# The down projection as seven block products with weight sums grown by accumulating loads

## The chip, the cores and the metric

The kernel runs on one core of a Trainium2 chip. Its time is the device time of one execution in microseconds (us). The kernel before was timed three times: median 670.09 us, from 669.1 to 670.38. The profile is of one further execution of 670.29 us; its span, from the first instruction to the last, is 668.5 us.

## The reference

One decoder layer in float32, 512 tokens by 1024 channels: two kinds of attention, a SwiGLU block of width 2816 and a last normalisation. The change concerns the last two lines:

```python
hn = rms_norm(h, norm2_g)
h = h + (silu(hn @ w_gate) * (hn @ w_up)) @ w_down      # (512 x 2816) @ (2816 x 1024)
return rms_norm(h, norm_f_g)
```

## The kernel before

TensorE multiplies numbers of a shortened float32 type (F32R). To keep float32 precision, each operand is split in two: a high part, a cast on ScalarE, and a low part, the difference, on VectorE. Three matmuls (high x high, high x low, low x high) then stand for one.

The gate and up products run first, in 22 units of 128 hidden channels (`first_part`, `second_part`, `third_part`, lines 716 to 746). Each unit already uses seven half-size products; its last one (the weights called `d`, line 744) adds into a bank that VectorE must have read before. The results lie in 22 tiles `zs`, 128 hidden channels by 512 tokens each: four tiles of four, whose names in the rows begin with `act`, and one of six named `h1t`. The operands of gate and up lie in the tiles `X10`, `X11`, `X20` and `X21`, which become free when the last unit has read them. The residual h1 waits in DRAM as `h1d`.

The down projection (lines 781 to 828) goes through the 22 row blocks in order. `down_step(k)` loads 128 rows of the weights (512 KB, SyncE), splits them (`split2`, 128x1024), splits `zs[k]` (`split_g`, 128x512), and issues eight cells, four token blocks by two column halves, each three matmuls of 128x128 by 128x512 into its own PSUM bank. All eight banks gather at once. The last four row blocks (`LAST`) are done cell by cell, so that a cell can be evicted (line 838: bank x 1/rms + h1), squared and, for the first half of a row, multiplied by the gain (line 842) while TensorE goes on. Then the row's root is taken (`rsqrt`) and the two halves are scaled and stored.

A scheduler orders the instructions of each engine from its own model of times; within `manual_schedule` the named engines keep the order of the code, here VectorE and ScalarE in the down projection. Each engine and each queue of transfers works in order, so a waiting instruction holds all behind it. Tiles with the same name share `bufs` buffers in turn: split weights `hl2` three, raw weights `raw2` six, `xe` and `xf` four, `w_hl` five, `w_raw` three.

Of the kernel before, what the change touches and what calls it, by code (L numbers as in the profile page):

```python
# [28 lines left out]
NJ = FFN // P  # L29
EPS = 1e-6  # L30
BIG = 1e30
TW = 640
WC = 512
RB = 32
LAST = 4
# [17 lines left out]
def tile_hybrid_layer(ctx: ExitStack, tc: tile.TileContext, xT, w_qk0, w_t, w_av, w_vb, w_o, w_gu, w_d,  # L53
                      rel, pos2, cw1, cb1, cw2, gT, gf_row, oh, cmask, out):
    nc = tc.nc
# [8 lines left out]
    def bank(tag):  # L64
        return psum.tile([P, 512], F32, name=tag, bufs=BANKS[tag])
# [476 lines left out]
    for step in PLAN.split():  # L542
        n, i = step[0], step[1:]
# [34 lines left out]
    def raw2():  # L578
        return ff.tile([P, 2, WC], F32, name="raw2", bufs=BUFS["raw2"])

    def split2(raw, hi, lo, w=None):

        if w is None:
            w = ff.tile([P, 2, 2, WC], F32R, name="hl2", bufs=BUFS["hl2"])
        copy(hi, w[:, 0], raw)
        tt(lo, w[:, 1], raw, w[:, 0].bitcast(F32), ALU.subtract)
        return w

    def raw1():
        return ws.tile([P, WC], F32, name="w_raw", bufs=BUFS["w_raw"])  # L590
# [151 lines left out]
    def third_part(j, u):  # L742
        y, z = u["y"], zs[j]
        product(u["A"], u["w"]["d"], X2, 4, False)
        tt("v", z[:, :HS], u["A"], y[:, :HS], ALU.mult)
        tt("v", z[:, HS:], z[:, HS:], y[:, HS:], ALU.mult)

    es = []
    for f in range(KT):
# [28 lines left out]
    third_part(NJ - 1, units[NJ - 1])  # L778


    GT = [ff.tile([P, n, S], F32R, name=tag, bufs=1) for n, tag in ((4, "X10"), (4, "X11"), (10, "X20"), (10, "X21"))]
    GH = [GT[0][:, k] for k in range(4)] + [GT[2][:, k] for k in range(10)] + [GT[3][:, k] for k in range(8)]
    GL = [GT[1][:, k] for k in range(4)]
    def w_down(k, w=None):
        raw = raw2()
        nc.sync.dma_start(raw, w_d[k * P:(k + 1) * P, :].rearrange("p (a n) -> p a n", a=2))
        return split2(raw, *ENG["d"], w)

    def split_g(k):
        if k % 4 == 0 and k:  # L790
            q = act.tile([P, 4, S], F32R, name=quads[k // 4 - 1]) if k < 20 else GT[3][:, 8:]
            GL.extend(q[:, i] for i in range(min(4, NJ - k)))
        copy("a", GH[k], zs[k])
        tt("v", GL[k], zs[k], GH[k].bitcast(F32), ALU.subtract)

    def down(ps, t, c, k, w):
        tk = slice(t * P, (t + 1) * P)
        mm3x(ps[c][t], GH[k][:, tk], GL[k][:, tk], w[:, :, c], slice(0, HD), k == 0, k == NJ - 1)

    ps = [[bank(n) for n in ("S", "S", "proj", "proj")], [bank(n) for n in ("PT", "PT", "PT", "O")]]  # L800
    def h1_back(t):
        if t % 2 == 0:
            h1r.append(ff.tile([P, 2, D], F32, name=("X10", "X11")[t // 2], bufs=1))
        nc.sync.dma_start(h1r[t // 2][:, t % 2], h1d[t])

    def cell(t, c):
        return h1r[t // 2][:, t % 2, c * HD:(c + 1) * HD]

    h1r, gf, ws_last, wx = [], [], [], []
    def down_step(k):  # L810
        if k < NJ - LAST:
            w = w_down(k)
        elif k < NJ - 2:
            ws_last.append(w_down(k))
        else:
            if k == NJ - 2:
                wx.append(ff.tile([P, 2, 2, 2, WC], F32R, name="X20", bufs=1))
            ws_last.append(w_down(k, wx[0][:, k - NJ + 2]))
        split_g(k)
        if k < NJ - LAST:  # L820
            for c in range(2):
                for t in range(NT):
                    down(ps, t, c, k, w)
        if k in (1, 2):
            gf.append(ff.tile([P, HD], F32, name="g", bufs=BUFS["g"]))
            nc.sync.dma_start(gf[-1], gf_row[:, (k - 1) * HD:k * HD].to_broadcast([P, HD]))
        if k in (7, 9, 11, 13):
            h1_back((k - 7) // 2)
# [4 lines left out]
    for t in range(NT):
        for c in range(2):
            for i, k in enumerate(range(NJ - LAST, NJ)):
                down(ps, t, c, k, ws_last[i])
            x = cell(t, c)
            nc.vector.scalar_tensor_tensor(out=x, in0=ps[c][t], scalar=nrstd_t[:, t:t + 1], in1=x, op0=ALU.mult,
                                           op1=ALU.add)
            square(t, c, x)  # L840
            if c == 0:
                tt(ENG["c"], x, x, gf[0], ALU.mult)
        rsqrt(slice(t, t + 1), rstd_t)
# [85 lines left out]
```

## Time and profile before

| | us |
|---|---|
| median of three runs | 670.09 |
| the profiled execution, and its span | 670.29, 668.5 |
| TensorE busy | 641.3 |
| VectorE busy | 477.3 |
| ScalarE busy | 352.9 |
| GpSimd busy | 144.3 |

Busy times are unions over the span and say nothing of which engine another waits for; that is read stage by stage. In the rows PE is TensorE, DVE VectorE, ACT ScalarE, POOL GpSimd and SP SyncE; L95 is line 95 of the kernel, and a helper's line stands for all its callers, so groups are told apart by tile names. Matmuls are pipelined: the duration shown for one (0.40 us) is longer than the distance to the next, and the distance is what counts. The same holds in small for VectorE, whose next instruction starts before the last has ended.

### The profile page before, as it was taken

How to read it: one execution, taken by the hardware profiler on the slowest of the kernel's cores; microseconds unless marked ns; L12 is line 12 of the kernel's file. 1: busy time of each engine (PE TensorE's matmuls, PEld its weight loads, DVE VectorE, ACT ScalarE, POOL GpSimd, SP SyncE). 2: the span in 40 equal slices, each digit the busy share in tenths (PEclk: the TensorE clock that was granted, in tenths of full speed). 3: DMA queues.
4: the chain of work that ended last, by engine and by line, in shares of the span. 5: the costliest groups of instructions: out<-in, count | busy, mean ns of one | idle time of the engine just before them, and what ended most of it. 6: DMA issues, size and time to landing. Idle time of an engine off the chain costs nothing.

```text
span 668.5 us, 11164 instructions
## 1 busy us (share of the span) xinstructions
PE 641.3 (96%) x3942; PEld 571.3 (85%) x3942; DVE 477.3 (71%) x994; ACT 352.9 (53%) x745; POOL 144.3 (22%) x184
## 2 busy tenths in 40 slices
PE   9999997999999999987999999999999999999995
PEld 6878887878878887866899999999999988888884
DVE  4458777678787679559899899999998724333355
ACT  5543565345775678558774455545545504222234
POOL 7635842153446645330000000000000000000000
PEclk9999999989999999888899999999999999999998
DMA  6666665446225640063433133323324417222003
GB/s 191 216 177 190 174 176 155 123 140 172 90 95 158 199 150 17 1 206 117 179 128 124 69 111 126 111 95 111 111 96 147 175 58 245 102 94 95 0 2 126
DMA packets 45316, 84.44 MB, mean 126 GB/s; under 512 B 6811, under 2 KB 10139, under 8 KB 45260
## 3 DMA queue, kind: packets, MB, share of 16 engines
q1 hardware_dynamic: 44684, 82.67, 39.1%
q10 hardware_dynamic: 576, 1.05, 0.4%
q8 instruction: 31, 0.51, 0.3%
q14 instruction: 25, 0.20, 0.1%
HBM read 68.45 MB, written 7.64 MB: 114 GB/s over the span
## 4 chain that ended last, share of the span: by engine, by line
PE 78%; DVE 8%; ACT 4%; DMA 4%; issue 3%; SPq 2%; POOL 1%; DVEq 0%; ACTq 0%; POOLq 0%
PE proj L89 8%; PE proj L91 8%; PE proj L90 8%; PE S L90 6%; PE S L89 6%; PE S L91 6%; PE PT L340 3%; PE PT L96 2%; PE PT L95 2%; PE PT L97 2%; PE O L356 2%; PE proj L96 2%; PE proj L95 2%; PE proj L97 2%; PE S L317 2%
## 5 line engine op out<-in xcount | busy, mean ns | idle before, releaser
L76 DVE TENSOR_TENSOR hl<-raw,hl 128x1024 fp32r<-128x1024 f32 x64 | 78.0, 1220 | 61.1 <-ACT hl L71 60.8
L71 ACT CAST hl<-raw 128x1024 fp32r<-128x1024 f32 x64 | 67.3, 1053 | 76.8 <-PE O L97 57.1
L84 POOL TENSOR_TENSOR w_hl<-w_raw,w_hl 128x512 fp32r<-128x512 f32 (+1 forms) x47 | 61.4, 1309 | 61.7 <-ACT w_hl L71 31.5
L71 ACT CAST w_hl<-w_raw 128x512 fp32r<-128x512 f32 (+2 forms) x76 | 43.3, 576 | 58.0 <-PE S L91 18.9
L325 ACT ACTIVATE P<-P,mn 128x512 f32<-128x512 f32 (+1 forms) x96 | 53.5, 559 | 13.3 <-DVE mn L323 13.0
L337 POOL TENSOR_SCALAR P<-P,den 128x512 f32<-128x512 f32 (+1 forms) x96 | 51.4, 554 | 41.4 <-DVE den L329 21.5
L76 DVE TENSOR_TENSOR PTl<-PT,PTh 128x512 fp32r<-128x512 f32 (+2 forms) x96 | 43.7, 482 | 10.2 <-ACT PTh L350 9.9
L323 DVE CUSTOM_DVE_ANT_0 P<-S,T 128x512 f32<-128x512 f32 (+1 forms) x96 | 44.0, 483 | 9.8 <-PE S L318 7.6
L89 PE MATMUL S<-X,hl 128*128 128x256 f32 x176 | 49.9, 284 | 0.7 <-ACT xf L721 0.7
L90 PE MATMUL S<-X,hl 128*128 128x256 f32 x176 | 50.0, 284 | 0.3 <-DVE X L76 0.3
L89 PE MATMUL S<-X,w_hl 128*128 128x256 f32 x176 | 49.7, 284 | 0.5 <-ACT xf L732 0.5
L350 ACT CAST PTh<-PT 128x512 fp32r<-128x512 f32 (+2 forms) x96 | 38.2, 426 | 22.7 <-PE PT L340 18.8
L90 PE MATMUL S<-X,w_hl 128*128 128x256 f32 x176 | 49.8, 283 | 0.0
L91 PE MATMUL S<-X,hl 128*128 128x256 f32 x176 | 49.7, 282 | 0.0
L91 PE MATMUL S<-X,w_hl 128*128 128x256 f32 x176 | 49.7, 283 | 0.0
L89 PE MATMUL proj<-xh,w_hl 128*128 128x512 f32 x112 | 45.6, 408 | 0.5 <-DVE va L282 0.4
L71 ACT CAST w_hl<-raw 128x512 fp32r<-128x512 f32 x45 | 27.3, 619 | 35.5 <-PE S L91 28.3
L90 PE MATMUL proj<-xl,w_hl 128*128 128x512 f32 x112 | 44.7, 399 | 0.0
L91 PE MATMUL proj<-xh,w_hl 128*128 128x512 f32 x112 | 44.6, 398 | 0.0
L84 DVE TENSOR_TENSOR w_hl<-w_raw,w_hl 128x512 fp32r<-128x512 f32 (+1 forms) x37 | 27.4, 747 | 15.7 <-ACT w_hl L71 14.4
L340 PE MATMUL PT<-ident,P 128*128 128x128 f32 x240 | 36.8, 277 | 0.8 <-POOL P L337 0.8
L89 PEld LDWEIGHTS S<-X,hl 128*128 128x128 f32 x176 | 33.9, 193 | 1.1 <-ACT xf L721 1.1
(316 smaller groups left out, 1965.1 us busy)
## 6 DMA issues: line engine op xcount, KB each, us to landing
raw<-in_w_gu_dram SPq DMA_DIRECT2D x46, 256.0 KB, 3.3
raw<-in_w_d_dram SPq DMA_DIRECT2D x22, 512.0 KB, 3.3
w_raw<-in_w_gu_dram SPq DMA_DIRECT2D x42, 256.0 KB, 2.7
w_raw<-in_w_t_dram SPq DMA_DIRECT2D x28, 256.0 KB, 2.8
T<-gd SPq DMA_DIRECT2D x64, 64.0 KB, 1.9
w_raw<-in_w_o_dram SPq DMA_DIRECT2D x16, 256.0 KB, 3.1
w_raw<-in_w_vb_dram SPq DMA_DIRECT2D x16, 140.0 KB, 2.2
Qb<-in_xT_dram SPq DMA_DIRECT2D x8, 256.0 KB, 2.8
```

Source lines behind the costliest of these rows:

```text
L71: nc.scalar.copy(out, in_)
L76: engines[e].tensor_tensor(out=out, in0=in0, in1=in1, op=op)
L84: engines[lo].tensor_tensor(out=w[:, 1, :n], in0=raw[:, :n], in1=w[:, 0, :n].bitcast(F32), op=ALU.subtract)
L89: nc.tensor.matmul(ps, w[:, 0, sl], xh, start=first, stop=False, skip_group_check=skip)
L90: nc.tensor.matmul(ps, w[:, 0, sl], xl, start=False, stop=False, skip_group_check=skip)
L91: nc.tensor.matmul(ps, w[:, 1, sl], xh, start=False, stop=last, skip_group_check=skip)
L95: nc.tensor.matmul(ps, xh, w[:, 0, sl], start=first, stop=False)
L323: nc.vector.tensor_tensor_reduce(out=pp, in0=sv, in1=T[:, S - w:], op0=ALU.add, op1=ALU.min, scale=1.0, scalar=3e38, accum_out=mn[:, t:t + 1])
L325: nc.scalar.activation(pp, pp, AF.Exp, bias=mn[:, t:t + 1], scale=-1.0, accum_out=den[:, t:t + 1])
L337: nc.gpsimd.tensor_scalar(pp, pp, den[:, t:t + 1], 1.0, op0=ALU.mult, op1=ALU.mult)
L340: nc.tensor.transpose(pv[:, kb * P:(kb + 1) * P], pp[:, kb * P:(kb + 1) * P], ident)
L350: nc.scalar.copy(ov[0], pv)
```

## The change

The 2816 hidden channels are cut into an upper and a lower eleven row blocks, the tokens and the output columns into halves. Instead of eight block products, seven are computed, one after the other, each over eleven row blocks for two token blocks and one column half (two banks). Their operands are sums of blocks. All sums on the side of the hidden values (`s1` to `s4`) are made in place on VectorE between the splits. The sums of the weights have plus signs alone. Most are made by loads that GpSimd issues and that add into the tile where it stands (`add_w`, `accum_op`); the rest (`t3`, and `t2` for the last two pairs of row blocks) are VectorE additions. The bank sums go into the residual tile `x0[2]` by evictions (`evict`) that add or subtract. Row blocks are taken in pairs, five pairs and a single one, a step each. TensorE and GpSimd now keep the code's order as well, and SyncE's loads are ordered by hand, too. The loads of the gain (`gf`) stand at their end.

```diff
-    ps = [[bank(n) for n in ("S", "S", "proj", "proj")], [bank(n) for n in ("PT", "PT", "PT", "O")]]
-        for k in range(NJ):
-            down_step(k)
+    HJ = NJ // 2
+    PAIRS = [slice(k, min(k + 2, HJ)) for k in range(0, HJ, 2)]
...
+    with tc.manual_schedule(engines={mybir.EngineType.SP}):
+        r11 = [raw2() for _ in PAIRS]
+        B11 = r11[:5] + [r11[5][:, 0:1]]
+        load_w(B11, 0, 0)
+        x0 = [ff.tile([P, n, WC], F32, name=tag, bufs=1)
+              for n, tag in ((4, "X10"), (4, "X11"), (10, "X20"), (10, "X21"))]
+        B21 = [x0[k // 2][:, 2 * (k % 2):2 * (k % 2) + 2] for k in range(4)] + [x0[2][:, 8:10], r11[5][:, 1:2]]
+        load_w(B21, 1, 0)
+        for t in range(NT):
+            nc.sync.dma_start(x0[2][:, 2 * t:2 * t + 2], h1d[t].rearrange("p (c n) -> p c n", c=2))
+        B22 = [x0[3][:, 2 * k:2 * k + 2] for k in range(5)] + [raw1()[:, None]]
+        load_w(B22, 1, 1)
+        B12 = [ws.tile([P, 2, WC], F32, name="w_hl", bufs=BUFS["w_hl"]) for _ in range(5)] + [raw1()[:, None]]
+        load_w(B12, 0, 1)
+        gf = [ff.tile([P, HD], F32, name="g", bufs=BUFS["g"]) for _ in range(2)]
...
+    def s1(k):
+        minus("v", A21[k], A21[k], A22[k])
...
+    def add_w(kh, ch):
+        def f(k):
+            for i in range(B11[k].shape[1]):
+                nc.gpsimd.dma_start(B11[k][:, i], rows_w(kh, ch, k, i), accum_op=ALU.add)
+        return f
+    def t2(k):
+        if k < 4:
+            add_w(1, 1)(k)
         else:
+            tt("v", B11[k], B11[k], B22[k], ALU.add)
+    def t3(k):
+        tt("v", B12[k], B12[k], B22[k], ALU.add)
...
+    products = [
+        (ps_a, A11, B11, True, (s3, add_w(0, 1)), [(ps_a, 0, 0)], []),
+        (ps_b, A12, B21, True, (s1,), [(ps_b, 0, 0)], [(0, 0), (1, 0)]),
+        (ps_c, A21, B11, True, (s2, t2), [(ps_c, 1, 1)], []),
+        (ps_a, A21, B11, False, (s4, add_w(1, 0)), [(ps_a, 0, 1, -1)], []),
+        (ps_c, A12, B22, False, (t3,), [(ps_c, 0, 1)], [(0, 1), (1, 1)]),
+        (ps_a, A11, B12, False, (), [(ps_a, 1, 1, -1), (ps_a, 1, 0)], [(2, 1), (3, 1)]),
+        (ps_b, A22, B11, True, (), [], [])]
...
+        copy("a", gh[:, :m], a)
+        minus("v", gl[:, :m], a, gh[:, :m].bitcast(F32))
+        copy("a", w[:, 0, :m], b)
+        minus("v", w[:, 1, :m], b, w[:, 0, :m].bitcast(F32))
...
+            parts = prepare(n, k)
+            for f in products[n][4]:
+                f(k)
+            if n == 6 and k >= 3:
+                last.append((k, *parts))
+            else:
+                for i in range(2):
+                    multiply(n, i, k, *parts)
+            if x == 0:
+                last_product(NJ - 1, units[NJ - 1])
+            if n and k == 2:
+                for e in products[n - 1][5]:
+                    evict(*e)
+            if n and k == 3:
+                for c in products[n - 1][6]:
+                    close(*c)
...
+        final(1)
+        square(3, 0, cell(3, 0))
+        store(2)
+        root(r3)
+        gain(3)
+        unroot(r3)
+        scale(3)
+        store(3)
```

What VectorE does in order changes most. In the middle of the down projection before, it alternates between the low part of hidden values (`act<-act,X`) and that of a row block's weights (`hl<-raw,hl`):

```order
L76 TENSOR_TENSOR act_6598<-act_3771,X_6453 128x512
L76 TENSOR_TENSOR hl_6627<-raw_6625,hl_6627 128x1024
L76 TENSOR_TENSOR act_6598<-act_3771,X_6453 128x512
L76 TENSOR_TENSOR hl_6658<-raw_6656,hl_6658 128x1024
L76 TENSOR_TENSOR act_6598<-act_3771,X_6453 128x512
L76 TENSOR_TENSOR hl_6689<-raw_6687,hl_6689 128x1024
```

In the third product of the change, from its fourth step on, `xf<-act,xe` and `hl<-raw,hl` are the splits of hidden values and weights, L848 and `raw<-raw,X` sums, and `X<-X,g` the two gain multiplies:

```order
L75 TENSOR_TENSOR xf<-act_3771,xe 128x512
L75 TENSOR_TENSOR hl_6843<-raw_6448,hl_6843 128x1024
L848 SCALAR_TENSOR_TENSOR act_3771<-h1t,act_3771 128x2x256
L75 TENSOR_TENSOR X_6464<-X_6464,g 128x512 x2
L75 TENSOR_TENSOR xf<-act_3772,xe 128x512
L75 TENSOR_TENSOR hl_6871<-raw_6449,hl_6871 128x1024
L848 SCALAR_TENSOR_TENSOR act_3772<-h1t,act_3772 128x2x256
L75 TENSOR_TENSOR raw_6449<-raw_6449,X_6465 128x1024
L75 TENSOR_TENSOR xf<-act_3772,xe 128x256
L75 TENSOR_TENSOR hl_6892<-raw_6450,hl_6892 128x512
```

Between two weight splits now stand sums, and the gain multiplies have moved from the end of the kernel into the middle of the stage.

SyncE's queue before, from the third weight block of the down projection on, with the two gain loads (`g<-in_gf_dram`) among the weights:

```order
L786 DMA raw_6529<-in_w_d_dram 128x1024
L786 DMA raw_6562<-in_w_d_dram 128x1024
L786 DMA raw_6593<-in_w_d_dram 128x1024
L786 DMA raw_6625<-in_w_d_dram 128x1024
L786 DMA raw_6656<-in_w_d_dram 128x1024
L826 DMA g<-in_gf_dram 128x512
L786 DMA raw_6687<-in_w_d_dram 128x1024
L786 DMA raw_6720<-in_w_d_dram 128x1024
L826 DMA g<-in_gf_dram 128x512
L786 DMA raw_6752<-in_w_d_dram 128x1024
```

And after, where `X_6462` to `X_6465` are X10, X11, X20 and X21:

```order
L813 DMA raw_6450<-in_w_d_dram 128x512
L813 DMA X_6462<-in_w_d_dram 128x512 x4
L813 DMA X_6463<-in_w_d_dram 128x512 x4
L813 DMA X_6464<-in_w_d_dram 128x512 x2
L813 DMA raw_6450<-in_w_d_dram 128x512
L832 DMA X_6464<-h1d 128x1024 x4
L813 DMA X_6465<-in_w_d_dram 128x512 x10
L813 DMA w_raw<-in_w_d_dram 128x512
L813 DMA w_hl<-in_w_d_dram 128x512 x10
L813 DMA w_raw<-in_w_d_dram 128x512
L839 DMA g<-in_gf_dram 128x512 x2
```

The gain loads have moved behind all weights, and from X_6464 on everything stands behind a load into X20.

## Rows read from the trace of the kernel before

**Rows 1.** Table by stretch: bounds, length, busy time and count by engine, clock, DMA share, GB/s.

```profile
520.00:540.00 20.00, 20.00 (x157) 19.38 (x156) 14.55 (x24) 10.04 (x17) 0.00 (x0) 1.00 0.51 179
560.00:580.00 20.00, 20.00 (x88) 16.19 (x87) 6.86 (x8) 6.27 (x8) 0.00 (x0) 1.00 0.55 193
600.00:620.00 20.00, 20.00 (x87) 16.23 (x86) 7.31 (x8) 6.22 (x8) 0.00 (x0) 1.00 0.22 79
660.00:668.50 8.50, 1.36 (x6) 0.75 (x4) 2.98 (x8) 1.83 (x6) 0.00 (x0) 0.74 0.33 123
```

**Rows 2.** TensorE in order of time: start, duration, engine, line, operation, tiles.

```profile
533.82 0.40 PE L95 MATMUL proj<-hl,X 128*128 128x512 f32 x1
534.06 0.40 PE L96 MATMUL proj<-hl,X 128*128 128x512 f32 x1
...
543.94 0.28 PE L89 MATMUL S<-X,w_hl 128*128 128x256 f32 x1
544.06 0.28 PE L90 MATMUL S<-X,w_hl 128*128 128x256 f32 x1
...
660.96 0.40 PE L97 MATMUL O<-X,X 128*128 128x512 f32 x1
```

**Rows 3.** VectorE in order of time, inside the gate and up products.

```profile
433.71 0.42 DVE L76 TENSOR_TENSOR g<-PT,xf 128x256 f32<-128x256 f32 x1
434.05 1.21 DVE L76 TENSOR_TENSOR hl<-raw,hl 128x1024 fp32r<-128x1024 f32 x1
435.18 0.68 DVE L76 TENSOR_TENSOR w_hl<-raw,w_hl 128x512 fp32r<-128x512 f32 x1
435.79 0.42 DVE L76 TENSOR_TENSOR act<-S,g 128x256 f32<-128x256 f32 x1
```

**Rows 4.** VectorE in order of time: an eviction and the instruction behind it.

```profile
658.62 0.75 DVE L838 SCALAR_TENSOR_TENSOR X<-proj,nrstd_t,X 128x512 f32<-128x512 f32 x1
659.29 0.74 DVE L846 SCALAR_TENSOR_TENSOR h<-X,rstd_t,g 128x512 f32<-128x512 f32 x1
```

**Rows 5.** VectorE groups by form from 540 us: count, busy us, mean ns.

```profile
L76 DVE TENSOR_TENSOR X<-X,g 128x512 f32<-128x512 f32 x4 | 2.8, 694 | 1.1 <-ACT g L657 1.0
```

**Rows 6.** ScalarE in order of time, at the seam.

```profile
534.02 0.37 ACT L732 COPY xf<-S 128x256 f32<-128x256 f32 x1 [1.94 <-PE S L91]
534.29 1.05 ACT L71 CAST hl<-raw 128x1024 fp32r<-128x1024 f32 x1
```

**Rows 7.** Queue share, loads (KB each, us to landing), and two single microseconds by stretch.

```profile
q1 hardware_dynamic: 44684, 82.67, 39.1%
...
raw<-in_w_gu_dram SPq DMA_DIRECT2D x46, 256.0 KB, 3.3
...
w_raw<-in_w_gu_dram SPq DMA_DIRECT2D x42, 256.0 KB, 2.7
...
565.00:566.00 1.00, 1.00 (x6) 0.82 (x5) 0.00 (x0) 0.00 (x0) 0.00 (x0) 1.00 1.03 418
570.00:571.00 1.00, 1.00 (x6) 0.82 (x5) 0.00 (x0) 0.00 (x0) 0.00 (x0) 1.00 0.93 360
```

**Rows 8.** VectorE groups by form, until 270 us, then from 330 us.

```profile
L84 DVE TENSOR_TENSOR w_hl<-w_raw,w_hl 128x512 fp32r<-128x512 f32 x21 | 19.5, 929 | 12.8 <-ACT w_hl L71 11.5 <-POOL oc L188 1.2
...
L76 DVE TENSOR_TENSOR w_hl<-raw,w_hl 128x512 fp32r<-128x512 f32 x41 | 27.8, 685 | 1.5 <-ACT w_hl L71 1.5
```

**Rows 9.** VectorE and ScalarE in order of time behind the last matmul.

```profile
661.40 0.75 DVE L838 SCALAR_TENSOR_TENSOR X<-O,nrstd_t,X 128x512 f32<-128x512 f32 x1 [0.48 <-PE O L97]
662.24 0.63 ACT L657 ACTIVATE g<-X 128x512 f32<-128x512 f32 x1 [2.05 <-DVE X L838]
...
663.00 0.16 DVE L662 SCALAR_TENSOR_TENSOR nv<-ss 128x1 f32<-128x1 f32 x1 [0.85 <-ACT g L657]
...
663.42 0.16 DVE L664 RECIPROCAL rstd_t<-nt 128x1 f32<-128x1 f32 x1 [0.27 <-ACT nt L663]
...
664.13 0.72 ACT L849 ACTIVATE X<-X,rstd_t 128x512 f32<-128x512 f32 x1 [0.74 <-DVE rstd_t L670]
```

More of the change, by code (lines that the diff above doesn't have):

```diff
@@ L34 @@
 RB = 32
-LAST = 4
 DELAY = 3
@@ L677, in second_norm @@
                 square(t, c, h1t[:, t, c * HD:(c + 1) * HD])
-        rsqrt(slice(0, NT), nrstd_t)
+        root(slice(0, NT))
+        unroot(slice(0, NT), nrstd_t)
         stat = bank("O")
@@ L728, in second_part @@
             Z = ff.tile([P, KT, S], F32, name="h1t", bufs=1)
+            zq.append(Z)
             zs.extend(Z[:, i] for i in range(NJ - 16))
@@ L768, in tile_hybrid_layer @@
     quads = ["act00", "act01", "act10", "act11"]
-    zs = [q[:, i] for tag in quads for q in [act.tile([P, 4, S], F32, name=tag)] for i in range(4)]
+    zq = [act.tile([P, 4, S], F32, name=tag) for tag in quads]
+    zs = [q[:, i] for q in zq for i in range(4)]
     second_part(0, units[0])
@@ L777, in tile_hybrid_layer @@
         second_part(j, units[j])
[L778 to L798, printed above, removed]
-    ps = [[bank(n) for n in ("S", "S", "proj", "proj")], [bank(n) for n in ("PT", "PT", "PT", "O")]]
@@ L801, in h1_back @@
[L801 to L804, printed above, removed]
-    def cell(t, c):
[L807 to L814, printed above, removed]
-        else:
[L816 to L828, printed above, removed]
@@ L830, in tile_hybrid_layer @@
-    with tc.manual_schedule(engines={mybir.EngineType.DVE, mybir.EngineType.Activation}):
-        for k in range(NJ):
-            down_step(k)
[L833 to L843, printed above, removed]
+    HJ = NJ // 2
@@ new lines, in tile_hybrid_layer, with hidden, rows_w @@
+    PAIRS = [slice(k, min(k + 2, HJ)) for k in range(0, HJ, 2)]
+    def hidden(half, rows):
+        v = []
+        for k in PAIRS:
+            j = k.start + (NJ - 10 if k.start < 10 else 1) * rows
+            v.append(zq[min(j // 4, 4)][:, j - 4 * min(j // 4, 4):][:, :k.stop - k.start, half * HS:(half + 1) * HS])
+        return v
+    A11, A12, A21, A22 = [hidden(h, r) for h in range(2) for r in range(2)]
+    def rows_w(kh, ch, n, i):
+        k = PAIRS[n].start
+        r = k + i + ((NJ - 10 if k < 10 else 1) if kh else 0)
+        return w_d[r * P:(r + 1) * P, ch * HD:(ch + 1) * HD]
@@ new lines, in load_w, with minus @@
+    def load_w(dst, kh, ch):
+        for n, k in enumerate(PAIRS):
+            for i in range(k.stop - k.start):
+                nc.sync.dma_start(dst[n][:, i], rows_w(kh, ch, n, i))
+    def minus(e, out, in0, in1):
+        tt(e, out, in0, in1, ALU.subtract)
+    ps_a, ps_c, ps_b = [[bank(n) for n in tags] for tags in (("PT", "O"), ("S", "S"), ("proj", "proj"))]
+    def cell(t, c):
+        return x0[2][:, 2 * t + c]
+    with tc.manual_schedule(engines={mybir.EngineType.SP}):
[13 more added lines that the diff above has]
+        gf = [ff.tile([P, HD], F32, name="g", bufs=BUFS["g"]) for _ in range(2)]
+        for c in range(2):
+            nc.sync.dma_start(gf[c], gf_row[:, c * HD:(c + 1) * HD].to_broadcast([P, HD]))
@@ new lines, in tile_hybrid_layer, with close, gain, scale @@
+    mrstd = ff.tile([P, NT], F32, name="mrstd", bufs=1)
+    nc.vector.tensor_scalar(mrstd, nrstd_t, -1.0, None, op0=ALU.mult)
+    def close(t, c):
+        square(t, c, cell(t, c))
+        if c == 0:
+            gain(t)
+    def gain(t):
+        tt(ENG["c"], cell(t, 0), cell(t, 0), gf[0], ALU.mult)
+    def scale(t):
+        x = cell(t, 0)
+        nc.scalar.activation(x, x, AF.Copy, scale=rstd_t[:, t:t + 1])
+        nc.scalar.dma_start(out[t * P:(t + 1) * P, :HD], x)
+    def store(t):
@@ new lines, in tile_hybrid_layer, with prepare @@
+    steps = [(n, k) for n in range(7) for k in range(len(PAIRS))]
+    def prepare(n, k):
+        a, b = products[n][1][k], products[n][2][k]
+        m = a.shape[1]
+        w = ff.tile([P, 2, 2, WC], F32R, name="hl2", bufs=BUFS["hl2"])
+        gh = ff.tile([P, 2, HS], F32R, name="xe", bufs=BUFS["xe"])
+        gl = ff.tile([P, 2, HS], F32R, name="xf", bufs=BUFS["xf"])
+        copy("a", gh[:, :m], a)
+        minus("v", gl[:, :m], a, gh[:, :m].bitcast(F32))
+        copy("a", w[:, 0, :m], b)
+        minus("v", w[:, 1, :m], b, w[:, 0, :m].bitcast(F32))
+        return gh, gl, w
@@ new lines, in multiply @@
+    def multiply(n, i, k, gh, gl, w):
+        ps, first = products[n][0], products[n][3]
+        s = slice(i * P, (i + 1) * P)
+        for j in range(PAIRS[k].stop - PAIRS[k].start):
+            start, stop = first and k == 0 and j == 0, PAIRS[k].start + j == HJ - 1
+            nc.tensor.matmul(ps[i], gh[:, j, s], w[:, 0, j], start=start, stop=False, skip_group_check=True)
+            nc.tensor.matmul(ps[i], gh[:, j, s], w[:, 1, j], start=False, stop=False, skip_group_check=True)
+            nc.tensor.matmul(ps[i], gl[:, j, s], w[:, 0, j], start=False, stop=stop, skip_group_check=True)
@@ new lines, in tile_hybrid_layer @@
+    last = []
+    with tc.manual_schedule(engines={mybir.EngineType.DVE, mybir.EngineType.Activation, mybir.EngineType.Pool,
+                                 mybir.EngineType.PE}):
+        for x, (n, k) in enumerate(steps):
+            if x == len(PAIRS):
+                nc.scalar.activation(nt[:, 0:1], ones[:, 0:1], AF.Sqrt)
+            parts = prepare(n, k)
+            if x == 2:
+                gated(NJ - 1, units[NJ - 1])
+            for f in products[n][4]:
[3 more added lines that the diff above has]
+            else:
+                for i in range(2):
+                    multiply(n, i, k, *parts)
[7 more added lines that the diff above has]
+                    close(*c)
@@ new lines, in final @@
+    def final(i):
+        x = cell(2 + i, 0)
+        nc.vector.scalar_tensor_tensor(out=x, in0=ps_b[i], scalar=nrstd_t[:, 2 + i:3 + i], in1=x, op0=ALU.mult,
+                                       op1=ALU.add)
+    r2, r3 = slice(2, 3), slice(3, 4)
+    with tc.manual_schedule(engines={mybir.EngineType.DVE, mybir.EngineType.Activation, mybir.EngineType.PE}):
+        root(slice(0, 2))
+        unroot(slice(0, 2))
+        for t in range(2):
+            scale(t)
+            store(t)
+        for x in last:
+            multiply(6, 0, *x)
+        final(0)
+        close(2, 0)
+        root(r2)
+        for x in last:
+            multiply(6, 1, *x)
+        unroot(r2)
+        scale(2)
+        final(1)
[6 more added lines that the diff above has]
+        store(3)
```

29 lines of the change are left out of this document (21 added, 8 removed).

## The prediction

> **What bounds the kernel now.** I read the table of time by stretch first. From 520 to 660 us TensorE is busy for all 20 us of each stretch at a granted clock of 1.00, the 2.4 GHz level; VectorE is busy for 7 to 15 of them and GpSimd for none [rows 1]. Then the instructions of TensorE in order of time. The first matmul of the down projection starts at 533.82, the next follows after 0.24 us, and the last starts at 660.96 [rows 2]; the matmuls of the gate and up products between them follow each other after 0.12 us. I call 533.8 time 0: at that point the second product of the last gate/up unit has just ended in both kernels. To the end of the last matmul (661.2) 127.4 us pass, and the work fills them: 22 row blocks x 8 cells x 3 = 528 matmuls x 0.2333 = 123.2, and 36 leftover matmuls of gate and up x 0.12 = 4.3. So the stage is bound by TensorE alone. Behind it stands the tail of normalisation and stores, 661.2 to 668.5 [rows 9]. The profiled execution took 670.3 us, 1.8 more than its span and 0.2 more than the median of the three timed runs (670.09); I sum against 670.3.
>
> **What goes.** Seven products of 11 row blocks x 2 halves x 3 = 462 matmuls replace 528. 66 x 0.2333 = 15.4 us leave TensorE, which is 15.4 off the end if nothing else comes late.
>
> **What VectorE gets instead.** A step is a pair of row blocks, TensorE 12 x 0.2333 = 2.80 us; the sixth step of a product is a single block, 1.40; a product is 15.4. Back to back, VectorE starts the next instruction 0.61 us after a 128x512 one, 1.13 after a 128x1024 one, 0.34 after a 128x256 one [rows 3], and 0.67 after an eviction, so 0.68 is taken for each SCALAR_TENSOR_TENSOR [rows 4]. Every step has the low part of the left block (0.61) and of the weights (1.13). With the sums this makes, per product:
> first, second and fourth: 5 x (0.61 + 1.13 + 0.61) + (0.34 + 0.61 + 0.34) = 13.0, with two evictions 14.4 in the second and fourth;
> third: its sums are SCALAR_TENSOR_TENSOR, 5 x 2.42 + 1.3 = 13.4; the two weight sums left on VectorE 1.13 + 0.61, two evictions 1.4 and two gain multiplies 1.2 [rows 5] give 17.8;
> fifth: weight sums 5 x 1.13 + 0.61 on top of the splits, and two evictions: 17.3;
> sixth and seventh: no sums, about 10 and their evictions.
> The first five come to 76.9 against 77.0 on TensorE. They balance, so what counts is where VectorE is late. The tile of split weights (hl2) has three buffers: ScalarE's cast of a step (1.05 us [rows 6]) waits until TensorE has left the step three before, and VectorE's 1.21 follows it. Where a single step lies between, VectorE can be ahead by at most 4.2 - 1.05 - 1.21 - 0.2 (for the matmul's end) = 1.7 us. So it enters the third product 1.7 ahead, needs 2.4 more than TensorE and is held once more by a buffer for about 0.4: TensorE waits about 1.2. The fourth gives back 1.0; the fifth takes 1.9: a wait of 0.9. The single steps ahead of the seventh product and of its last half cost 0.2 and 0.7.
> At the seam, the last unit's final product follows its third one directly on TensorE, where before 22 down matmuls lay between them, each waiting for VectorE to read the bank between them. VectorE gets to that read about 0.7 us after the third product's end: the copy of the second product is on ScalarE at 534.02 and a weight cast behind it to 535.3 [rows 6], then VectorE has 1.21 + 0.69 + 0.42 queued. Together 0.7 + 1.2 + 0.9 + 0.9 = 3.7 us of waits on TensorE. With the full durations of the rows instead of the start-to-start times (0.685, 1.21, 0.75) the same walk gives about 8.5; less than 0 is excluded, since no matmul gets shorter. I take 3.7, since the spacing rows are what a full queue does.
>
> **Transfers.** SyncE's loads stand in one queue, and the pair of gain loads (line 839) last. All from X20 on wait until the last unit's final product has left X20, at 7.8. The first gain multiply stands in VectorE's order in the third product's fourth step. TensorE enters that product at 7.8 + 5 steps (12.6) + 15.4 = 35.8 and VectorE 1.7 earlier, so the gain is wanted at 34.1 + 0.7 + 0.4 + 3 x 2.42 + 1.4 = 43.8. All of VectorE is queued behind it, and its lead is used up there, so TensorE waits as long. From 7.8 on SyncE has to bring 34 quarter megabytes (256 KB) up to the first gain load. At the best rate of the trace, 418 GB/s in one microsecond, one such unit takes 0.63 us; 360 GB/s at a share of 0.93 makes 0.68; the mean over queue 1 (82.67 MB in 39.1% of the span) 0.83 [rows 7]. Beside them GpSimd issues accumulating loads, of which no row exists: 11 during the first product and 8 during the third, 256 KB each. At least one costs what a plain load costs, 0.63. At most, if nothing of two overlaps, what a lone one takes to land, 2.7 to 3.3 [rows 7]. An accumulating load has to fetch the tile as well as the HBM rows, so I take two units, 1.3, nearer the plain row. About 11 of them compete before 43.8 (5 and 6): 34 + 22 = 56 units x 0.65 = 36.4, landing 2.5: the gain arrives at 46.8, 3 us late. With 0.63 and one unit each it is in time (0); with 0.83 and two it is 13 late. I take 3. The Trainium skill (Collectives: The Full Stack, The bandwidth ceiling) says that a reduce-scatter is half as fast as an all-gather because the add in the DMA engine needs two source reads, not because adding costs anything. By that the 1.3 would stand; no run here shows an accumulating load.
> The accumulating loads' own deadline is looser: the first product's sums are used 12 steps later, the third product's 6 steps later.
>
> **Tail.** The last chain keeps its steps (evict, square, root, reciprocal, correction, reciprocal, scale, store [rows 9]). A gain multiply now stands between the sum and the first reciprocal: that started 0.42 after the sum and will start about 0.16 + 0.61 after it: 0.4 more. The store of the tile before fits into the 1.6 us between eviction and sum.
>
> **Sum.** 670.3 - 15.4 + 3.7 + 3.0 + 0.4 = 662.0 us.
>
> **Rivals.**
> 1. All loads in time (accumulating loads near the plain price): 662.0 - 3.0 = 659.0. For it: two of the stretches of before show only 193 and 79 GB/s [rows 1]. Against: three times the number of loads.
> 2. Accumulating loads too slow, the slower side. The last of the first 19 must have landed when ScalarE casts its weights in the fourth product, about time 59 (52.4 + 3 steps of 2.8, less cast and split). From -4, when the first split ends, the engines have SyncE's 43 units (8 into X10 and X11, 34 and the second gain load), 28 us, and 19c. With 2 us to land, 28 + 19c has to fit into 61: c up to 1.75 us; the gain of 11.3 (659.0 without other waits) is gone at c = 2.3. At 2.7, the landing time of a plain load taken as its price [rows 7], the delay is 18: 677 us. At 3.3 it is 688. For it: no row shows this operation, and GpSimd also has to issue each one. Against: SyncE's plain loads overlap freely.
> 3. VectorE slowed beside GpSimd. In the first 270 us, where GpSimd computes, a 128x512 subtraction from two tiles in SBUF takes 929 ns; later, with GpSimd idle, 685 [rows 8]. Should issuing transfers do the same, by 1.36, the five products cost VectorE 105 against 77 and the end lies near 685; a factor near 1.17 eats the gain. The Trainium skill (SBUF — State Buffer, Who interferes with whom) says that a VectorE instruction with two SBUF inputs contends with a GpSimd instruction that reads SBUF and not with one that only writes, and infers that descriptor generation needs the write side. By that the factor is 1 and the sum stands; the 929 agrees with the first half, and no row shows the second.
> 4. The gain is eaten by many small waits (8.5 on VectorE and 3 for the loads): 667.
>
> **How the numbers follow.** Forecast with its neighbours up to rival 4 (660 to 668): 0.47. Rival 1: 0.25. Rival 2: 0.20, of which 0.03 with a delay under 10 us. Rival 3: 0.05. Something else, either way: 0.03. The likeliest one's own range is 660 to 668. The range of 8 in 10 runs from 657.5, a little under rival 1, to 677, the middle of rival 2. What this kernel's timing can tell from no change is about 0.2%, 1.3 us. Faster than that: 0.47 + 0.25 and 0.03 from rival 2 = 0.75; within it 0.04; slower 0.21.
>
> **What would show it.** 462 down matmuls, still 0.233 apart. TensorE's idle time in the stage between 4 and 9 us, ended by the split on VectorE, most of it in the third and fifth products. A VectorE wait of some us for the gain load at the first gain multiply; none means rival 1. Splits and sums at 0.69 and 1.21 us: longer means rival 3. Casts on ScalarE in the third and fourth products that wait for a transfer mean rival 2. I am wrong if TensorE's idle time is over 12 us, or if the stretch ahead of 533 has changed length, which no step here explains.

## The result, and the profile after

The changed kernel takes 666.54 us (median of 20 runs, 663.69 to 672.42) against 670.60 (20 runs, 668.38 to 672.12). The ratio is 0.9949, interval 0.9936 to 0.9963: faster by 0.5%, where the sum said 1.2% (662.0). The direction and the range held; the size did not.

| | before | after | forecast |
|---|---|---|---|
| median, us | 670.60 | 666.54 | 662.0 |
| profiled execution | 670.3 | 669.47 | |
| its first down matmul starts at | 533.82 | 535.88 | 533.8 |
| from there to the end of the last matmul ("the stage") | 127.4 | 123.4 | 118.7 |
| from there to the end of the span | 7.3 | 8.3 | 7.7 |

The profiled execution after is 2.9 us above its median; its first down matmul comes 2.1 us later than in the profile before. In the eight experiments below the first down matmul starts between 532.07 and 538.49, though the seven of them other than the first change nothing ahead of it; so this is taken as spread between executions and no effect of the change. Below, stage lengths of profiled executions are compared, and medians for the whole. A stage is counted to the start of its last matmul and one pace (0.23 us) more; after the change these two matmuls are

```profile
535.88 0.39 PE L928 MATMUL PT<-hl,xe 128*128 128x512 f32 x1
...
659.07 0.39 PE L930 MATMUL proj<-hl,xf 128*128 128x512 f32 x1
```

The 20 runs after spread over 8.7 us, those before over 3.7. Of the changed kernel there is one profile, so how much of its wait differs from run to run is not shown.

The table by stretch of the changed kernel, with two stretches of [rows 1] first, then five at the place of the loss (length, busy time of TensorE, its weight loads, VectorE, ScalarE and GpSimd with counts, granted clock, DMA share, GB/s):

```profile
560.00:580.00 20.00, 20.00 (x90) 16.57 (x89) 18.22 (x26) 12.56 (x21) 6.85 (x8) 1.00 1.08 326
600.00:620.00 20.00, 20.00 (x90) 16.57 (x89) 19.76 (x26) 11.43 (x17) 7.91 (x9) 1.00 0.85 142
...
575.00:580.00 5.00, 5.00 (x23) 4.14 (x23) 3.72 (x6) 3.88 (x9) 3.26 (x4) 1.00 1.11 266
580.00:585.00 5.00, 2.24 (x10) 1.50 (x9) 0.00 (x0) 2.04 (x3) 0.17 (x1) 1.00 1.10 261
585.00:590.00 5.00, 0.00 (x0) 0.00 (x0) 0.80 (x2) 0.00 (x0) 0.00 (x0) 0.75 0.85 192
590.00:595.00 5.00, 2.72 (x6) 2.15 (x7) 5.00 (x8) 0.00 (x0) 0.00 (x0) 0.50 0.00 2
595.00:600.00 5.00, 5.00 (x18) 4.00 (x17) 5.00 (x8) 2.57 (x4) 1.75 (x2) 0.73 0.12 14
```

VectorE, which was busy 7 of 20 us, is now busy 18 to 20, and the DMA engines went from a share of 0.55 to 1.08 between 560 and 580. From 582.2 to 589.2 neither TensorE nor VectorE works, and TensorE starts again at 592.3. VectorE's instructions in order of time (start, duration, what it waited for) say why:

```profile
578.04 0.68 DVE L848 SCALAR_TENSOR_TENSOR act<-h1t,act 128x512 f32<-128x512 f32 x1
589.20 1.29 DVE L75 TENSOR_TENSOR X<-X,g 128x512 f32<-128x512 f32 x2 [10.48 <-DMA g<-in_gf_dram]
590.41 0.68 DVE L75 TENSOR_TENSOR xf<-act,xe 128x512 fp32r<-128x512 f32 x1
```

VectorE waits 10.48 us for the gain load at the first gain multiply of the third product, with the splits for TensorE queued behind. TensorE in order of time, the answer to [rows 2]:

```profile
581.85 0.39 PE L928 MATMUL S<-hl,xe 128*128 128x512 f32 x1
592.28 0.80 PE L929 MATMUL S<-hl,xe 128*128 128x512 f32 x1 [10.04 <-DVE hl L75]
...
593.30 0.63 PE L928 MATMUL S<-hl,xe 128*128 128x512 f32 x1
...
598.12 0.39 PE L928 MATMUL S<-hl,xe 128*128 128x512 f32 x1
...
598.80 0.39 PE L928 MATMUL PT<-hl,xe 128*128 128x512 f32 x1
599.03 0.39 PE L929 MATMUL PT<-hl,xe 128*128 128x512 f32 x1
...
599.48 0.39 PE L928 MATMUL PT<-hl,xe 128*128 128x512 f32 x1
```

Two more things stand here. Behind the idle stretch the granted clock is at 0.50, the 1.2 GHz level, and from 592.28 to 598.12 fourteen matmuls start 0.42 us apart on the mean, until the clock is at 1.00 again: 14 x (0.417 - 0.227) = 2.7 us. And at full clock the down matmuls follow each other after 0.2267 us (three from 598.80 to 599.48), not after the 0.2333 of [rows 2].

The gain loads stand last in SyncE's queue. SyncE's issues in order of time (start, time until the last one of the row was issued):

```profile
544.78 0.44 SPq L813 DMA_DIRECT2D raw<-in_w_d_dram  x1
545.26 1.88 SPq L832 DMA_DIRECT2D X<-h1d  x4
548.76 16.84 SPq L813 DMA_DIRECT2D X<-in_w_d_dram  x10
...
566.51 6.43 SPq L813 DMA_DIRECT2D w_hl<-in_w_d_dram  x10
...
573.94 1.20 SPq L839 DMA_DIRECT2D g<-in_gf_dram  x2
```

They are issued from 573.9 on, and the first lands 15 us later. The queues in the stretches 544 to 590, 566 to 570 and 582 to 586 (packets, MB, share of the 16 engines' time in that stretch; q1 is SyncE's, q0 GpSimd's accumulating loads):

```profile
q1 hardware_dynamic: 4738, 9.67, 58.0%
q0 software_dynamic: 2219, 4.02, 47.6%
...
q1 hardware_dynamic: 865, 1.58, 105.3%
...
q0 software_dynamic: 288, 0.52, 70.8%
q1 hardware_dynamic: 288, 0.52, 39.7%
```

From 544 to 590 the engines are full (58.0 + 47.6 = 106%; these are summed times of packets, and packets overlap in part, so that shares can pass 100%). A quarter megabyte (256 KB, 0.262 MB) of plain load took 58.0% x 46 us / (9.67 / 0.262) = 0.72 us of them, an accumulating one 47.6% x 46 / (4.02 / 0.262) = 1.43. Alone, q1 moved 395 GB/s (1.58 MB in 4 us). Side by side each queue got 288 packets: SyncE's loads fell to 131 GB/s as soon as GpSimd's were there. The Trainium skill (DMA: Bandwidth & Descriptors, Queues, rings and completion order) says that an engine goes round between the queues it has work for, packet by packet; the equal counts agree.

Durations on VectorE while GpSimd issues, by form (544 to 600), against [rows 3, 8]; and the gain multiplies, against [rows 5]:

```profile
L75 DVE TENSOR_TENSOR hl<-raw,hl 128x1024 fp32r<-128x1024 f32 x9 | 11.0, 1218 | 0.5 <-ACT hl L70 0.5
L75 DVE TENSOR_TENSOR xf<-act,xe 128x512 fp32r<-128x512 f32 x11 | 7.5, 683 | 0.8 <-ACT xe L70 0.8
...
L75 DVE TENSOR_TENSOR X<-X,g 128x512 f32<-128x512 f32 x4 | 2.7, 689 | 11.3 <-DMA g<-in_gf_dram 10.5 <-ACT g L656 0.8
```

They are what they were (1.21 and 0.685 us). Over the whole stage, the 6 splits of 128x1024 and the 11 of 128x512 that ran mostly while GpSimd was issuing took 1.215 and 0.681 us on the mean. Issuing 30 accumulating loads, 0.88 us each on GpSimd, did not slow VectorE.

### The profile page after: what moved, and what is told of

Same layout as the page of the kernel before. It is cut to its first block, busy times and chain, and to the rows that moved or that the text cites. A ratio compares the mean times of both kernels' runs of the same rounds, so it can differ in the third digit from the quotient of the medians.

```text
span 667.6 us, 11272 instructions
## 1 busy us (share of the span) xinstructions
PE 628.0 (94%) x3876; PEld 560.3 (84%) x3876; DVE 530.5 (79%) x1072; ACT 379.5 (57%) x785; POOL 170.0 (25%) x214
## 4 chain that ended last, share of the span: by engine, by line
PE 70%; DMA 11%; DVE 9%; ACT 5%; issue 3%; SPq 1%; POOL 1%; ACTq 0%; DVEq 0%; POOLq 0%
PE proj L88 8%; PE proj L90 8%; PE proj L89 8%; PE S L88 6%; PE S L89 6%; PE S L90 6%; PE PT L339 3%; DMA g<-in_gf_dram 2%; DMA X<-h1d 2%; PE S L316 2%; PE O L355 2%; PE O L358 2%; PE S L317 2%; DMA w_raw<-in_w_t_dram 1%; DMA X<-in_w_d_dram 1%
## 5 line engine op out<-in xcount | busy, mean ns | idle before, releaser
L859 POOL DMA_DIRECT2D raw<-in_w_d_dram x30 | 26.5, 1041 | 287.8 <-DVE hl L75 280.8
L70 ACT CAST hl<-raw 128x1024 fp32r<-128x1024 f32 (+1 forms) x69 | 70.5, 1022 | 40.5 <-PE S L930 16.7
L75 DVE TENSOR_TENSOR hl<-raw,hl 128x1024 fp32r<-128x1024 f32 (+1 forms) x69 | 81.2, 1178 | 3.0 <-ACT hl L70 2.9
L75 DVE TENSOR_TENSOR PTl<-PT,PTh 128x512 fp32r<-128x512 f32 (+2 forms) x96 | 43.8, 482 | 10.2 <-ACT PTh L349 9.7
L88 PE MATMUL proj<-xh,w_hl 128*128 128x512 f32 x112 | 46.1, 412 | 1.2 <-DVE va L281 1.1
L90 PE MATMUL proj<-xh,w_hl 128*128 128x512 f32 x112 | 45.6, 407 | 0.0
```

The lines of the kernel that those rows point to most:

```text
L88: nc.tensor.matmul(ps, w[:, 0, sl], xh, start=first, stop=False, skip_group_check=skip)
L90: nc.tensor.matmul(ps, w[:, 1, sl], xh, start=False, stop=last, skip_group_check=skip)
L859: nc.gpsimd.dma_start(B11[k][:, i], rows_w(kh, ch, k, i), accum_op=ALU.add)
```

## The experiments

All times are medians with the ratio to the kernel before, run on the same chip (670.49 for the first four, 671.13 for the last four, 670.60 for the changed kernel itself; between these groups the ratios are the fairer comparison).

| run | us | ratio, interval | stage, us | TensorE's waits over 0.4 us |
|---|---|---|---|---|
| changed kernel | 666.54 | 0.9949, 0.9936 to 0.9963 | 123.4 | 0.5, 10.0 |
| gain load first | 659.52 | 0.9842, 0.9817 to 0.9867 | 116.2 | 0.5, 3.0, 0.9, 0.6 |
| gain multiply later | 656.64 | 0.9789, 0.9768 to 0.9811 | 111.3 | 0.5, 0.6 |
| plain loads | 657.46 | 0.9807, 0.9787 to 0.9827 | 112.5 | 0.5, 0.8, 0.6 |
| filler | 668.24 | 0.9961, 0.9937 to 0.9986 | 123.1 | 0.5, 2.8 behind the filler, 1.0, 0.6 |
| gain load behind h1 | 657.14 | 0.9797, 0.9775 to 0.9819 | 112.5 | 0.5, 0.7, 0.6 |
| fifth sums by DMA | 655.53 | 0.9764, 0.9744 to 0.9784 | 109.9 | 0.5 |
| bank change by three | 656.26 | 0.9783, 0.9757 to 0.9810 | 111.3 | 0.5, 0.6 |
| fifth sums and seam | 654.39 | 0.9747, 0.9721 to 0.9772 | 109.7 | none |

### The gain load first

```
         load_w(B11, 0, 0)
+        gf = [...]
+        for c in range(2):
+            nc.sync.dma_start(gf[c], ...)
         x0 = [...]
...
         load_w(B12, 0, 1)
-        gf = [...]
-        for c in range(2):
-            nc.sync.dma_start(gf[c], ...)
```

> Edit: SyncE issues the two gain loads right behind the loads of the first weight block instead of last; nothing else moves. Theory A (the gain load, last in a saturated queue, is what was late): VectorE's wait of 10.5 us at the first gain multiply is gone, TensorE's idle 10.2 us in the third product with it, and the granted clock stays at 1.00 there, so the 13 matmuls behind it that took 0.43 instead of 0.227 us cost nothing (2.65 us in the changed kernel's profile). TensorE then waits about 1 us in the third product for VectorE. 666.5 - 10.2 - 2.6 + 1 = about 655, between 653.5 and 657.5. Theory B (the loads as a whole are late, and the gain only happened to be the first to be wanted): the wait moves to the accumulating sums of the third product, which ScalarE wants in the fourth, or to the last loads of the sixth product's weights; 660 to 666, with a ScalarE cast waiting for a DMA.

659.52: the wait for the gain went, but 659.5 is outside what theory A gave (653.5 to 657.5). A new wait had come. VectorE at the first eviction of the second product:

```profile
560.06 0.75 DVE L875 SCALAR_TENSOR_TENSOR X<-PT,nrstd_t,X 128x512 f32<-128x512 f32 x1 [3.62 <-DMA X<-h1d]
```

And SyncE's issues:

```profile
524.44 12.99 SPq L829 DMA_DIRECT2D g<-in_gf_dram  x2
537.53 9.04 SPq L813 DMA_DIRECT2D X<-in_w_d_dram  x10
```

The first of the two gain loads is issued at 524.4, the second 13 us later: its buffer is still that of the last unit but one, whose last read on VectorE comes only then. The loads into X10 behind it leave the queue at 537.5, 5.3 us after the first down matmul (532.22); in the run with the later multiply they left it 4.1 us before that matmul (530.94 against 535.04). So the h1 loads were late in their turn. Theory A named the wait, but not what a blocked load does to those behind it in the queue.

### The gain multiply later

```
     def close(t, c):
         square(t, c, cell(t, c))
-        if c == 0:
+        if (c == 0) == (t > 1):
             gain(t)
```

> Edit: the gain loads stay last in SyncE's queue; the gain multiplies of the first two row blocks move from the fourth step of the third product to the fourth step of the sixth. Theory A: nothing wants the gain before it lands, so the time is that of the kernel with the early gain load within 1 us (about 655), possibly 0.5 better, since 1.2 us of VectorE's work leaves the third product, where it is late, for the sixth, where it has time. Theory B as for the early gain load: 660 to 666. If this one is fast and the early load is not, the place of the load delays others.

656.64, 9.9 under the changed kernel and 1.6 above the 655 expected, with the queue untouched. TensorE's waits from 525 on (total, times, longest), and a stretch at the place of the loss:

```profile
PE S L929 <- DVE hl L75: 0.6, 1, 0.6
PE S L88 <- DVE h1t L75: 0.5, 1, 0.5
```
```profile
585.00:590.00 5.00, 5.00 (x24) 4.14 (x23) 5.00 (x7) 2.92 (x4) 3.51 (x4) 1.00 1.11 196
```

The DMA engines are as full as they were (1.11), and neither TensorE nor VectorE waits for a load: the loads as a whole are in time, one multiply was too early for its load. Theory B falls. How close the rest is shows on ScalarE: it waits once, 1.9 us until 589.2, for an accumulating load, and TensorE does not feel it.

### Plain loads

```
-                nc.gpsimd.dma_start(B11[k][:, i], rows_w(kh, ch, k, i), accum_op=ALU.add)
+                nc.gpsimd.dma_start(B11[k][:, i], rows_w(kh, ch, k, i))
```

> Edit: the 30 accumulating loads become plain loads of the same rows into the same tiles, from the same queue and in the same order; the sums of weights are left out, so the values are not the reference's. The gain stays last in SyncE's queue. In the changed kernel's profile the accumulating loads take 1.35 us of the 16 DMA engines for 256 KB and the plain ones 0.74. Theory A (their price is what makes the gain late): 19 of them precede the gain, 19 x 0.6 = 11.6 us of the engines go, the gain is in time or at most 2 us late, and the time is 655 to 659. Rival C (an accumulating load costs about a plain one; SyncE's own 43 loads and the even sharing between the two queues make the gain late): the wait stays over 6 us and the time 663 to 667.

657.46, and VectorE does not wait for the gain. Its gain multiplies, and below them GpSimd's queue with plain loads, alone on the engines (576 to 580):

```profile
577.51 1.29 DVE L75 TENSOR_TENSOR X<-X,g 128x512 f32<-128x512 f32 x2
```
```profile
q0 software_dynamic: 222, 0.74, 52.0%
```

52.0% x 4 us / (0.74 / 0.262) = 0.74 us for a quarter megabyte, against the 1.43 of the accumulating loads above. So it is the accumulation that doubles the price, not the queue, and rival C falls. The gain load was late by the extra time of these loads, 0.7 us for each of up to 19.

### The filler

```
+            if (n, k) == (2, 4):
+                for i in range(32):
+                    nc.tensor.matmul(ps_b[0], before[0][:, 0, :P], before[2][:, 0, 0], start=True, stop=True, ...)
+            before = parts
```

> Edit: 32 matmuls of the same shape, whose results are overwritten, stand on TensorE ahead of the fifth step of the third product, where it waits 10 us for VectorE; the wait itself stays. Theory A1: the granted clock stays at 1.00, and what the fall to 0.50 cost comes back in full: 13 matmuls x 0.2 = 2.6 us, so 664. Theory A2: the clock stays, but behind the wait VectorE is busy without a gap (589 to 620 in the profile), and TensorE at full speed waits for it: by the ends of its splits the fourth product starts 1.2 us earlier, not 2.6: 665.3. Rival: the clock falls in spite of the filler, or the filler outlasts the wait: 666.5 or more.

668.24: no gain; its interval overlaps that of the changed kernel, and it lies above the 664 and 665.3 of A1 and A2. A stretch of the wait, and TensorE in order of time:

```profile
585.00:590.00 5.00, 5.00 (x24) 4.14 (x23) 0.00 (x0) 0.00 (x0) 0.00 (x0) 1.00 1.11 265
```
```profile
584.45 7.42 PE L945 MATMUL proj<-hl,xe 128*128 128x512 f32 x32
591.71 0.39 PE L928 MATMUL S<-hl,xe 128*128 128x512 f32 x1
594.93 0.50 PE L929 MATMUL S<-hl,xe 128*128 128x512 f32 x1 [2.84 <-DVE hl L75]
...
600.29 0.50 PE L929 MATMUL PT<-hl,xe 128*128 128x512 f32 x1 [0.98 <-DVE hl L75]
```

Neither reason of the rival is the cause: the clock stayed at 1.00 (its mean from 525 to 662), as A1 and A2 said, and 2.8 us of the wait were left behind the filler. But TensorE at full clock only meets VectorE's backlog sooner: it waits 1.0 us at the start of the fourth product and 0.6 in the fifth, where the changed kernel has no wait over 0.4. The second matmul of the fourth product starts 61.8 us behind the first down matmul (538.49) instead of 63.2 (599.03 - 535.88), near the 1.2 earlier of A2; at the end of the stage 0.3 is left of it. So the fall of the clock cost 2.7 us where it happened and next to nothing at the end.

### The gain load behind h1

```
         for t in range(NT): the loads of h1d
+        gf = [...]
+        for c in range(2):
+            nc.sync.dma_start(gf[c], ...)
         B22 = [...]
...
         load_w(B12, 0, 1)
-        gf = [...]
-        for c in range(2):
-            nc.sync.dma_start(gf[c], ...)
```

> Edit: the two gain loads stand behind the four loads of h1 (22 of the second block's quarter megabytes and more still come after them); the gain multiplies stay in the third product. With the gain load ahead of everything, the second of its tiles waited until 537 for VectorE's last read of the buffer, and eight weight loads behind it left SyncE's queue 6.6 us later than without it. Theory A: here that wait is over long before, so neither the gain nor h1 is late; TensorE waits only for VectorE, 0.8 in the fourth product and 1 in the fifth as in the kernel with plain loads: 657 to 658.5. Rival: any place ahead of the last pushes h1 or B22 past their use, and the time stays near 659.5 or above.

657.14, within 0.5 us of the later multiply and of plain loads; TensorE's only wait in the fourth product:

```profile
PE PT L929 <- DVE hl L75: 0.7, 1, 0.7
```

With the multiplies where the change put them, the place of two loads alone is worth 9.4 us by the medians (10.2 by the ratios). This is the changed kernel with all loads in time, and its stage of 112.5 us the yardstick for the other terms.

### The fifth product's sums by DMA

```
-    def add_w(kh, ch):
+    def add_w(kh, ch, B=B11):
...
-        (ps_c, A12, B22, False, (t3,), [(ps_c, 0, 1)], [(0, 1), (1, 1)]),
+        (ps_c, A12, B22, False, (add_w(1, 1, B12),), [(ps_c, 0, 1)], [(0, 1), (1, 1)]),
```

> Edit on top of the later gain multiply: the fifth product's sums of weights, 11 row blocks that VectorE adds, become accumulating loads from GpSimd's queue. Theory: VectorE loses 5 x 1.13 + 0.61 = 6.3 us there, so that TensorE's waits for it in the fifth and sixth products (0.76 + 0.11 + 0.11 + 0.18 + 0.11 over the pace of 0.227) go: 656.6 - 1.3 = 655.3, 654.5 to 656. The DMA engines are at a share of 0.01 to 0.4 from 600 on, and the sums are used 15 us after they are issued. Rival: VectorE is not what ends those waits, or the added loads hold up the fourth product's sums, which go through the same queue: 656.6 or more.

655.53, as the theory had it (655.3); the stage is 1.4 us shorter than with the later multiply alone. The intervals of the two overlap, so it is the profile that shows it: of TensorE's waits only the seam is left, and VectorE is no longer busy without a gap. The second view is a row of its table by stretch, the third its queue from 600 to 610, where accumulating loads are alone on the engines.

```profile
PE S L88 <- DVE h1t L75: 0.5, 1, 0.5
```
```profile
600.00:610.00 10.00, 10.00 (x46) 8.29 (x45) 9.10 (x12) 5.83 (x9) 8.18 (x10) 1.00 1.11 198
```
```profile
q0 software_dynamic: 1089, 1.97, 110.7%
```

The last row prices them without SyncE's loads beside them: 110.7% x 10 us / (1.97 / 0.262) = 1.47 us, at 197 GB/s.

### The bank change by three

```
-    def multiply(n, i, k, gh, gl, w):
+    def multiply(n, i, k, gh, gl, w, only=None):
...
-                for i in range(2):
-                    multiply(n, i, k, *parts)
+                for j in range(parts[0].shape[1]):
+                    for i in range(2):
+                        multiply(n, i, k, *parts, j)
```

> Edit on top of the later gain multiply: within a step the two row blocks are taken one after the other for both halves, so that TensorE changes the PSUM bank after 3 matmuls instead of 6, as the kernel before did; work, operands and everything else stay. It asks why the down matmuls of the changed kernel follow each other after 0.2267 us where those before took 0.2333. Theory P1 (the change of bank costs): the pace goes to 0.2333, 462 x 0.0067 = 3.1 us, so 659.7. Theory P2 (it is something else, the place of the operands for one): the pace stays 0.2267 and the time 656.6.

656.26, and the pace stayed:

```profile
573.01 0.39 PE L930 MATMUL S<-hl,xf 128*128 128x512 f32 x1
...
573.69 0.39 PE L930 MATMUL S<-hl,xf 128*128 128x512 f32 x1
```

0.68 for three matmuls, with the bank changing after each three. P1 falls. What sets the pace stays open. The kernel before already had both paces at a granted clock of 1.00: matmuls of the same shape in its early projections start 0.226 us apart (eight distances from 50.18 to 51.99), those of its down projection 0.2333.

```profile
50.18 0.39 PE L89 MATMUL proj<-xh,w_hl 128*128 128x512 f32 x1
...
51.99 0.39 PE L91 MATMUL proj<-xh,w_hl 128*128 128x512 f32 x1
```

The place of the operands, P2's example, was not tried.

### The fifth product's sums and the seam

```
-            if x == 0:
+            if x == 1:
                 last_product(NJ - 1, units[NJ - 1])
...
-            if x == 2:
+            if x == 3:
                 gated(NJ - 1, units[NJ - 1])
```

> Edit on top of the fifth product's sums by accumulating loads: the last gate/up product and its gating stand one step later (behind the second step of the down projection). Theory: the 0.5 us that TensorE waits at the seam for VectorE's read of the bank go; 0.5 under the kernel without this edit: 654.8. Rival: the tile for h1 and B22 comes free 2.7 us later, so the h1 loads are late at the second product's evictions as in the kernel with the gain load first (3.6 us late there, 6.6 us after a later issue): 0 to 1 us slower than without it.

654.39, 1.1 under the run without this edit; the intervals overlap and the stage is 0.2 shorter, so more than that is not shown. Both theories were at work: the seam's 0.5 is gone and no wait of TensorE over 0.4 us is left, while VectorE now waits for h1:

```profile
DVE X L875 <- DMA X<-h1d: 1.0, 1, 1.0
```

This version has the lowest median, 2.5% under the kernel before.

## Why the prediction was wrong in size

**The term that failed is the 3.0 us for the gain load, and in it the count of accumulating loads that compete with it.** Its place, its victim and the way it reaches TensorE were right: the last load of SyncE's queue, the fourth step of the third product, all of VectorE behind it. It measured 10.5. The gain was wanted at time 42.8 (forecast 43.8) and came at 53.3 (46.8). The working said "about 11 of them compete before 43.8 (5 and 6)". From 544 to 590 GpSimd's queue moved 4.02 MB, 15.3 accumulating loads. The sum for the gain starts at 7.8 as if the engines were empty then. But six of the first product's loads had been issued by 540.7, and four of these, like some of SyncE's loads into X11, were still on their way when X20 came free at 543.9; and all eight of the third product's were issued by 580.2 and shared the engines packet by packet with the gain load.

The price was nearly right, 1.43 us against 1.3 taken, and so was the factor of two that the reading of two sources had suggested. The plain load took 0.72, not 0.65. In the prediction's form, at the measured 106% to 108% share: 36.9 x 0.72 / 1.08 + 15.3 x 1.43 / 1.08 = 24.6 + 20.3 = 44.9 us, where I had 36.4 and 2.5 of landing. Of the 6.0 more for the accumulating loads, 4.3 x 1.3 = 5.6 is the count.

The prediction had the better count at hand: its walk for rival 2 starts at -4, with 43 loads of SyncE and all 19 of GpSimd. At the prices taken this gives 28 + 19 x 1.3 - 4 + 2.5 = 51.2, 7 us late instead of 3. Its case of 13 us late is near the 10.5 by luck: it rests on a dearer plain load (0.83), not on more loads in flight. Of the signs named, a wait for the gain came, but the waits on TensorE came to 10.5 us (forecast 4 to 9), nearly all in the third product.

**The clock** was not in the sum. A wait of 10 us on TensorE was followed by 2.7 us of slow matmuls; the filler shows that this was covered by VectorE's backlog, so the omission cost nothing here.

**The pace** was taken as 0.2333 for the 462 that stay. It is 0.2267: 462 x 0.0067 = 3.1 us in our favour, unforeseen and unexplained. The prediction's "no matmul gets shorter" was wrong here. That it hid part of the miss is luck. The run with all loads in time took 657.1, where rival 1 said 659.0.

**VectorE's waits, 3.7.** In the run with the gain load behind h1, 112.5 - 462 x 0.2267 - 36 x 0.12 = 3.5 us remain. The size was right, the places partly: by the gaps between starts 0.7 at the seam (0.7 said), 1.1 in the fourth product instead of the third, 1.3 in the fifth and sixth; the rest is the slower pace of the first steps. In the changed kernel itself they come to 1.2, because the slow matmuls behind the wait let VectorE get ahead, as the filler shows from the other side.

**The tail, 0.4.** The last chain, against [rows 9]:

```profile
660.57 0.63 ACT L656 ACTIVATE g<-X 128x512 f32<-128x512 f32 x1 [0.41 <-DVE X L958]
...
661.32 0.16 DVE L660 SCALAR_TENSOR_TENSOR nv<-ss 128x1 f32<-128x1 f32 x1 [0.42 <-ACT g L656]
...
662.00 0.16 DVE L666 RECIPROCAL rstd_t<-nt 128x1 f32<-128x1 f32 x1
...
662.70 0.72 ACT L891 ACTIVATE X<-X,rstd_t 128x512 f32<-128x512 f32 x1 [0.98 <-DVE rstd_t L672]
```

From the sum to the reciprocal it takes 0.68 us instead of 0.42, so the gain multiply there costs 0.3, not 0.4; from the last eviction (659.49) to the scale 3.2 instead of 2.7. The step was right; another 0.5 us lies in the last stores (4.9 us from the scale to the end, 4.4 before).

**The rivals.** Rival 3 is refuted by the durations above, and with it the Trainium skill's inference (SBUF — State Buffer, Who interferes with whom) is borne out: issuing from GpSimd did not hold up VectorE's instructions with two inputs. Rival 2's mechanism, late sums in the fourth product, did not decide: 1.43 is under its 2.3. Its sign, a cast on ScalarE that waits for a transfer, came only in runs where the wait for the gain was gone, 0.3 to 2.4 us once in a run (1.9 with the later multiply), and in none of them did TensorE wait for it. Rival 4's 667 is near the time measured and for another reason: one wait, not many.

In sum, for the stage: 118.7 forecast, + 7.2 (TensorE's gap of 10.2 instead of 3.0), + 2.7 clock, - 3.1 pace, - 2.5 fewer small waits = 123.0; measured 123.4.

## What to carry to other kernels

Before a load is moved to the end of a queue, count everything that will be in flight on all queues from its issue to its use: also what was issued earlier and has not landed, not only what is issued in that time. Where an engine that feeds others in order has to wait for a late operand, moving the one instruction can be worth as much as cheaper traffic (here two multiplies, 656.6, against plain loads, 657.5). Loads moved ahead of others must not themselves wait for a buffer, or the whole queue inherits the wait.

## What the runs showed of the hardware

- An accumulating load of 256 KB from HBM into SBUF took 1.43 us of the 16 DMA engines beside plain loads and 1.47 alone, a plain one 0.72 and, on the same queue, 0.74; alone the rate was 197 GB/s against 395.
- With both queues full each got the same number of packets (288 and 288 in 4 us), so SyncE's plain loads fell from 395 to 131 GB/s.
- Behind ten idle microseconds TensorE's granted clock stood at 0.50, and its matmuls started 0.43 us apart before it came back to 1.00; with 32 more matmuls in that time, and 2.8 us idle behind them, it stayed at 1.00.
- Accumulating loads issued from GpSimd, 0.88 us each, did not slow VectorE's subtractions of two tiles in SBUF: 0.683 and 1.218 us beside them, 0.685 and 1.21 before.
- Matmuls of one shape at a granted clock of 1.00 ran at two paces: 0.2333 us in the down projection of the kernel before, 0.226 in its early projections and 0.2267 in most of the stage after. Changing the PSUM bank after every three matmuls instead of six did not bring the slower pace back (0.68 us for three).
